# The inverse of a chunked scan gets a scheduling priority on VectorE, ScalarE and the queues, and the clock that merges its streams gets other pauses

## The chip, the cores and the metric

The kernel runs on one core of a Trainium2 chip. The metric is the device time of one execution in microseconds (us), from the first to the last instruction, with what lies around them. Times of a program are medians over several runs.

## What is computed

The reference is two layers of a block with 256 latent and 256 context tokens (512 columns here), width 1024. Each layer is a SwiGLU half step, a mixer of three branches (grouped attention, RWKV-7 in both directions, neighbourhood attention) and a second SwiGLU half step. The change touches the RWKV branch alone. Cut to what matters:

```python
def rwkv_scan(state0, xs, emit):
    def step(state, inp):
        r_t, w_t, k_t, v_t, a_t, b_t = inp
        sa = jnp.einsum('zbhvk,zbhk->zbhv', state, a_t)
        state = state * w_t[..., None, :] + sa[..., :, None] * b_t[..., None, :] + v_t[..., :, None] * k_t[..., None, :]
        out = jnp.einsum('zbhvk,zbhk->zbhv', state, r_t) if emit else None
        return state, out
    return lax.scan(step, state0, xs)
```

It runs for two directions z, 8 heads of 64. In layer 0 all 512 tokens give an output, in layer 1 the 256 latent tokens alone.

## The kernel before, in words

The scan is computed in chunks of 64 tokens (8 per direction), and the 8 heads as four pairs, ct = 0 to 3 (here "blocks"). For each block and direction the kernel makes scaled keys and rates (`rwkv_dir`, L1119 to L1177, mostly VectorE, DVE), Gram matrices of 64x64 (`gram`, L1205), the inverse of one minus a triangular matrix per chunk, and then the chain over the 8 chunks (`chain_steps`, L1365), which is the only part that runs chunk after chunk.

The inverse has two parts. `blocks16` (L1270) takes the 16x16 diagonal blocks through DRAM into another layout, solves them with 30 short instructions on DVE (L1284, L1286), and takes them back. `inverse` (L1293) then doubles the block size twice: for each direction z it builds T and W (L1310, two instructions), and runs a sequence that goes back and forth between TensorE (PE) and DVE: PE `ps_x` into X (DVE L1327), PE `ps_it` into T (L1331), PE `ps_iw` into W (L1334), then PE 32x32 groups `ps_x2` (L1345, in the rows `ps_x`) and `ps_w2` (L1354, in the rows `ps_w`), each copied by ScalarE (ACT, L1240) and DVE (L1242) halves. All PSUM results of one direction share one or two banks, so the next group also needs the one before to be read out.

Around it lie other works. `rwkv_proj` (L1045) projects keys k, values v and r of the next blocks: 24 matmuls `ps_p` each (L330 to L332), whose weights are split in two parts by ACT and DVE (`phi`, `plo`, L336 and L337), and whose result `shift` (L892 to L895) reads out. `rwkv_unit` (L1052) squares k on ACT (L1063), sums the squares on PE (`ps_ss`, L392) and normalises. `fill` pops a quantum of three matmuls `ps_gate` (L845 to L847) of a projection that is needed only after the scan; its weights come with `wload` (ACT L320, DVE L321).

The order on PE is written by hand. Each of these works is a Python generator that writes instructions and yields (cost, pause): the PE time of what it wrote and the time in which it expects its input not to be there. The class `Streams` keeps a clock, takes the first stream in the list whose pause is over, and otherwise one fill quantum, for which it adds 0.9 (layer 0) or 0.65 (layer 1) to the clock. PE executes in that order, and waits where an input is late. After the last chain the fill quanta that are left are written (all but 64 in layer 0 and 16 in layer 1), so the sum of PE work does not depend on the pauses. The quantum order is fixed, too.

```python
        streams = [chains(), inverses(), keys(), outs(), preps(), projections()]
        with self.tc.manual_schedule(engines={mybir.EngineType.PE}):
            while mix.step(streams):
                pass
        self.fill(len(self.fq) - left)
```

The other engines and the DMA queue have no order by hand: the scheduler of the framework orders them from the data dependencies, its own estimates and a priority, which is the place in the program. `self.prio(n)` (L339) gives what is written under it the priority of something written n instructions earlier. Before, of the scan only `chains()` writes under such a priority (200).

Of the kernel before, what the change touches and what calls it, by code (L numbers as in the profile page):

```python
# [7 lines left out]
F32 = mybir.dt.float32  # L8
F32R = mybir.dt.float32r
AF = mybir.ActivationFunctionType  # L10
# [4 lines left out]
P = 128  # L15
# [4 lines left out]
NT = SEQ + CTX  # L20
# [5 lines left out]
C = 64  # L26
# [86 lines left out]
class Program:  # L113
# [788 lines left out]
    def rwkv(self):  # L902
# [94 lines left out]
        def keys():  # L997
            for ct in range(4):
                yield from until("gram", ct)
                yield from until("chain", ct - 1)  # L1000
                yield from self.keys(sts[ct]["z"][1])
                done["keys"] = ct

        def inverses():
            for ct in range(4):
                yield from until("gram", ct)
                yield from blocks(ct)
                done["inverse"] = ct

        def chains():  # L1010
            for ct in range(4):
                yield from until("inverse", ct)
                yield from until("keys", ct)
                with self.prio(200):
                    po = self.bank("po", [P, NCH, C], "ps_oo")
                steps = self.chain_steps(sts[ct], po)
                while True:
                    with self.prio(200):
                        try:
                            s, *said = next(steps)  # L1020
                        except StopIteration:
                            break
                    if s == NCH // 2:
                        done["half"] = ct
                    yield said
                with self.prio(200):
                    sts[ct]["o"] = self.rp.tile([P, NT], F32, tag="yf", name="yf", bufs=1)
                    nc.scalar.activation(out=sts[ct]["o"][:, tok], in_=po.rearrange("p j t -> p (j t)")[:, tok],
                                         func=AF.Copy)
                done["chain"] = ct  # L1030

        def outs():
            yield from until("rates", 0)
            for ct in range(4):
                yield from until("chain", ct)
                yield from self.rwkv_out(ct, sts[ct])
                done["out"] = ct

        streams = [chains(), inverses(), keys(), outs(), preps(), projections()]
        with self.tc.manual_schedule(engines={mybir.EngineType.PE}):  # L1040
            while mix.step(streams):
                pass
# [2 lines left out]
    def rwkv_proj(self, ct, st, which):  # L1045

        i, full = dict(k=(T_RK, FULL), v=(T_RV, FULL), r=(T_R, self.tok))[which]
        pt = yield from self.proj(i + ct, full)
        st[which] = self.shift(i - T_R + ct, full, pt)
        yield 0.0, 2.5  # L1050

    def rwkv_unit(self, ct, st):  # L1052

        nc, l, tok, need = self.nc, self.l, self.tok, self.need
        pr = self.rwp[:, l]
        st["lora"] = self.rp.tile([P, 2, P], F32, tag="lora", name="lora", bufs=1)
        nc.sync.dma_start(out=st["lora"], in_=self.A["lora"][l, ct][:, 0:2, :])
        g2 = self.rp.tile([P, P], F32, tag="g2", name="g2")
        nc.sync.dma_start(out=g2, in_=self.A["lora"][l, ct][:, 2, :])
        yield lambda: "k" in st  # L1060
        k = st["k"]
        sq = self.t()
        nc.scalar.activation(out=sq, in_=k, func=AF.Square, scale=pr[:, 4, ct:ct + 1])  # L1063
        bc = yield from self.rstd_steps([sq], 4, self.hsel, 1.0, 1e-12)
        kk = self.rp.tile([P, NT], F32, tag="kk", name="kk", bufs=1)
        nc.vector.scalar_tensor_tensor(out=kk, in0=k, scalar=pr[:, 4, ct:ct + 1], in1=bc, op0=ALU.mult, op1=ALU.mult)
        st.update(g2=g2, kk=kk)
        yield 1.1, 0.2
# [31 lines left out]
    def rwkv_low(self, ct, st):  # L1100

        nc, l = self.nc, self.l
        lora = st["lora"]
        st["z"] = [None, None]
        st["pc"] = self.rp.tile([P, NCH, 2], F32, tag="pc", name="pc", bufs=2)
        st["low"] = [[], []]
        for i, (x, w) in enumerate(((self.wdt, 0), (self.adt, 2))):
            pts = [self.bank("aux", [P, NT], "ps_w") for _ in range(2)]
            for z in range(2):
                rows = slice(64 * z, 64 * z + 64)  # L1110
                nc.tensor.matmul(pts[z], lora[rows, i, :], x[rows, :], start=True, stop=True)
            for z in range(2):
                t = self.t()
                nc.scalar.activation(out=t, in_=pts[z], func=AF.Tanh, scale=0.5,
                                     bias=self.wah[:, l, w + z, ct:ct + 1])
                st["low"][z].append(t)
            yield 2.1, 0.0

    def rwkv_dir(self, ct, z, st):  # L1119

# [171 lines left out]
    def inverse(self, st, z, tag):  # L1292
# [4 lines left out]
        d, dr = st["z"][z], st["dr"]  # L1297
        G = d["G"]
        if z == 1:
            yield 0.0, 2.5  # L1300

        def ch(a):
            return a.rearrange("p (j t) -> p j t", t=C)
# [13 lines left out]
        def mm(name, a, b):  # L1317
            pt = self.bank(tag, [P, NCH, C], name)
            for j in range(NCH):
                for p, h in enumerate(halves):  # L1320
# [5 lines left out]
        X = ch(self.it())  # L1326
        nc.vector.tensor_tensor(out=X, in0=px, in1=self.mlev[:, z, :].unsqueeze(1).to_broadcast([P, NCH, C]),  # L1327
                                op=ALU.mult)
        yield 1.15, 1.6
        pt = mm("ps_it", lambda p, h, j: W[h, j, :], X)  # L1330
        nc.vector.tensor_tensor(out=T, in0=T, in1=pt, op=ALU.add)  # L1331
        yield 1.15, 0.0
# [318 lines left out]
```

## Time and profile before

| | |
|---|---|
| Median of 3 runs | 2953.67 us (2942.95 to 2959.11) |
| Profiled execution, its own time | 2946.8 us |
| Its span, first to last instruction | 2945.0 us |
| Mean granted TensorE clock | 0.953 |
| Busy PE, DVE, ACT, POOL | 93%, 58%, 36%, 11% |

A busy share of PE counts time in which a matmul was in flight. An idle stretch of PE ends when the last input of its next instruction arrives; the profile names the instruction that delivered it. The granted clock is 1.0 at 2.4 GHz and 0.5 at 1.2 GHz; TensorE has these two levels, and a mean between them tells the mix.

### The profile page before, as it was taken

How to read it: one execution, taken by the hardware profiler on the slowest of the kernel's cores; microseconds unless marked ns; L12 is line 12 of the kernel's file. 1: busy time of each engine (PE TensorE's matmuls, PEld its weight loads, DVE VectorE, ACT ScalarE, POOL GpSimd, SP SyncE). 2: the span in 40 equal slices, each digit the busy share in tenths (PEclk: the TensorE clock that was granted, in tenths of full speed). 3: DMA queues.
4: the chain of work that ended last, by engine and by line, in shares of the span. 5: the costliest groups of instructions: out<-in, count | busy, mean ns of one | idle time of the engine just before them, and what ended most of it. 6: DMA issues, size and time to landing. Idle time of an engine off the chain costs nothing. (4 is left out here: it accounts for less than half of the span.)

```text
span 2945.0 us, 48446 instructions
## 1 busy us (share of the span) xinstructions
PE 2733.0 (93%) x19654; PEld 2224.2 (76%) x19654; DVE 1716.8 (58%) x2855; ACT 1064.0 (36%) x1928; POOL 311.4 (11%) x306
## 2 busy tenths in 40 slices
PE   7999998898899899999999999999788899898998
PEld 5788886666667666697888878888666667877898
DVE  4667346666642357657762476533577774386664
ACT  3222234332322346442222332222543333464543
POOL 0000022111100101220000200001211110022000
PEclk9999998898899999999999999999888889999999
DMA  7655342221123533445553365433332113644654
GB/s 276 200 192 164 108 128 71 67 61 48 46 79 124 166 114 93 123 131 186 182 167 106 124 207 175 134 107 118 96 87 57 50 58 96 200 140 138 211 176 150
DMA packets 207616, 379.74 MB, mean 129 GB/s; under 512 B 80033, under 2 KB 110369, under 8 KB 207393
## 3 DMA queue, kind: packets, MB, share of 16 engines
q1 hardware_dynamic: 207392, 376.65, 41.1%
q8 instruction: 154, 2.52, 0.4%
q14 instruction: 70, 0.57, 0.1%
HBM read 342.50 MB, written 33.03 MB: 128 GB/s over the span
## 5 line engine op out<-in xcount | busy, mean ns | idle before, releaser
L320 ACT ACTIVATE whi<-raw 128x1024 fp32r<-128x1024 f32 (+1 forms) x399 | 415.2, 1041 | 1109.9 <-PE ps_o L331 297.3
L321 DVE TENSOR_TENSOR wlo<-raw,whi 128x1024 fp32r<-128x1024 f32 (+1 forms) x399 | 498.6, 1250 | 501.5 <-ACT whi L320 495.5
L330 PE MATMUL ps_o<-hh,whi 128*128 128x512 f32 (+1 forms) x770 | 268.8, 349 | 0.0
L253 DVE SCALAR_TENSOR_TENSOR acc<-araw,cs,acc 128x1024 f32<-128x1024 f32 x210 | 260.6, 1279 | 13.5 <-DMA araw<-in_w_ada 13.2
L845 PE MATMUL ps_gate<-uh,whi 128*128 128x512 f32 (+1 forms) x672 | 265.2, 395 | 3.2 <-ACT fg L851 2.7
L332 PE MATMUL ps_o<-hh,wlo 128*128 128x512 f32 (+1 forms) x770 | 267.9, 348 | 0.0
L331 PE MATMUL ps_o<-hl,whi 128*128 128x512 f32 (+1 forms) x770 | 266.6, 346 | 0.0
L330 PE MATMUL ps_fg<-uh,whi 128*128 128x512 f32 (+1 forms) x704 | 256.6, 364 | 7.6 <-ACT uh L336 3.8
L332 PE MATMUL ps_fg<-uh,wlo 128*128 128x512 f32 (+1 forms) x704 | 254.4, 361 | 6.2 <-DVE wlo L321 6.2
L332 PE MATMUL ps_fu<-uh,wlo 128*128 128x512 f32 (+1 forms) x704 | 251.9, 358 | 4.6 <-DVE wlo L321 4.6
L331 PE MATMUL ps_fg<-ul,whi 128*128 128x512 f32 (+1 forms) x704 | 253.6, 360 | 0.1
L330 PE MATMUL ps_fu<-uh,whi 128*128 128x512 f32 (+1 forms) x704 | 251.0, 356 | 0.9 <-ACT whi L320 0.9
L331 PE MATMUL ps_fu<-ul,whi 128*128 128x512 f32 (+1 forms) x704 | 250.9, 356 | 0.0
L846 PE MATMUL ps_gate<-ul,whi 128*128 128x512 f32 (+1 forms) x672 | 243.2, 362 | 0.0
L847 PE MATMUL ps_gate<-uh,wlo 128*128 128x512 f32 (+1 forms) x672 | 242.5, 361 | 0.0
L330 PEld LDWEIGHTS ps_fg<-uh,whi 128*128 128x128 f32 x704 | 135.2, 192 | 39.3 <-ACT whi L320 12.0
L330 PEld LDWEIGHTS ps_o<-hh,whi 128*128 128x128 f32 x770 | 144.7, 188 | 20.4 <-ACT whi L320 1.7
L331 PEld LDWEIGHTS ps_o<-hl,whi 128*128 128x128 f32 x770 | 144.5, 188 | 20.1
L332 PEld LDWEIGHTS ps_o<-hh,wlo 128*128 128x128 f32 x770 | 144.7, 188 | 18.2
L845 PEld LDWEIGHTS ps_gate<-uh,whi 128*128 128x128 f32 x672 | 132.0, 196 | 32.5 <-issue 5.7
L332 PEld LDWEIGHTS ps_fg<-uh,wlo 128*128 128x128 f32 x704 | 134.9, 192 | 27.1 <-DVE wlo L321 7.6
L332 PEld LDWEIGHTS ps_fu<-uh,wlo 128*128 128x128 f32 x704 | 133.7, 190 | 25.9 <-DVE wlo L321 7.2
(299 smaller groups left out, 5193.3 us busy)
## 6 DMA issues: line engine op xcount, KB each, us to landing
raw<-in_ffn_wi SPq DMA_DIRECT2D x176, 512.0 KB, 3.6
araw<-in_w_ada SPq DMA_DIRECT2D x144, 512.0 KB, 3.8
raw<-in_w_in SPq DMA_DIRECT2D x92, 512.0 KB, 3.7
raw<-in_ffn_wo SPq DMA_DIRECT2D x70, 448.0 KB, 3.3
raw<-in_ffn_wo SPq DMA_DIRECT2D x35, 512.0 KB, 3.5
pd<-fg SPq DMA_DIRECT2D x52, 256.0 KB, 2.0
raw<-in_w_branch SPq DMA_DIRECT2D x24, 512.0 KB, 3.7
raw<-in_w_in SPq DMA_DIRECT2D x44, 256.0 KB, 2.7
```

Of the source, the lines that this page charges most:

```text
L253: nc.vector.scalar_tensor_tensor(out=a, in0=raw, scalar=c, in1=a, op0=ALU.mult, op1=ALU.add)
L320: nc.scalar.activation(out=hi[:, :m], in_=r, func=AF.Copy)
L321: self.lo = nc.vector.tensor_tensor(out=lo[:, :m], in0=r, in1=hi[:, :m].bitcast(F32), op=ALU.subtract)
L330: nc.tensor.matmul(pt, wh, xh[k], start=first and k == 0, stop=False)
L331: nc.tensor.matmul(pt, wh, xl[k], start=False, stop=False)
L332: nc.tensor.matmul(pt, wl, xh[k], start=False, stop=last and k == n - 1)
L845: nc.tensor.matmul(pt, wh, xh, start=k == 0, stop=False)
L846: nc.tensor.matmul(pt, wh, xl, start=False, stop=False)
L847: nc.tensor.matmul(pt, wl, xh, start=False, stop=k == KD - 1)
```

## The change

It does three things. The streams `chains()` and `inverses()` are wrapped in `urgent`, so that all they write has a priority 600 and 400 instructions earlier (before: 200 for the chains, none for the inverse). Five pauses of the merging clock become longer, and one is added: after the square of k (`rwkv_unit`), 9.0 for the first block and 2.0 for others; `rwkv_proj` 5.0 for 2.5; the second group of `rwkv_low` 0.5 for 0.0; the start of the second direction's inverse 4.0 for 2.5; after X in the inverse 2.2 for 1.6. No arithmetic is added, removed or altered. Line numbers of the changed kernel are two or three higher in these functions.

```diff
--- before.py
+++ after.py
@@ -1007,26 +1007,28 @@
                 yield from blocks(ct)
                 done["inverse"] = ct
 
+        def urgent(n, stream):
+
+            while True:
+                with self.prio(n):
+                    try:
+                        said = next(stream)
+                    except StopIteration:
+                        return
+                yield said
+
         def chains():
             for ct in range(4):
                 yield from until("inverse", ct)
                 yield from until("keys", ct)
-                with self.prio(200):
-                    po = self.bank("po", [P, NCH, C], "ps_oo")
-                steps = self.chain_steps(sts[ct], po)
-                while True:
-                    with self.prio(200):
-                        try:
-                            s, *said = next(steps)
-                        except StopIteration:
-                            break
+                po = self.bank("po", [P, NCH, C], "ps_oo")
+                for s, *said in self.chain_steps(sts[ct], po):
                     if s == NCH // 2:
                         done["half"] = ct
                     yield said
-                with self.prio(200):
-                    sts[ct]["o"] = self.rp.tile([P, NT], F32, tag="yf", name="yf", bufs=1)
-                    nc.scalar.activation(out=sts[ct]["o"][:, tok], in_=po.rearrange("p j t -> p (j t)")[:, tok],
-                                         func=AF.Copy)
+                sts[ct]["o"] = self.rp.tile([P, NT], F32, tag="yf", name="yf", bufs=1)
+                nc.scalar.activation(out=sts[ct]["o"][:, tok], in_=po.rearrange("p j t -> p (j t)")[:, tok],
+                                     func=AF.Copy)
                 done["chain"] = ct
 
         def outs():
@@ -1036,7 +1038,7 @@
                 yield from self.rwkv_out(ct, sts[ct])
                 done["out"] = ct
 
-        streams = [chains(), inverses(), keys(), outs(), preps(), projections()]
+        streams = [urgent(600, chains()), urgent(400, inverses()), keys(), outs(), preps(), projections()]
         with self.tc.manual_schedule(engines={mybir.EngineType.PE}):
             while mix.step(streams):
                 pass
@@ -1047,7 +1049,7 @@
         i, full = dict(k=(T_RK, FULL), v=(T_RV, FULL), r=(T_R, self.tok))[which]
         pt = yield from self.proj(i + ct, full)
         st[which] = self.shift(i - T_R + ct, full, pt)
-        yield 0.0, 2.5
+        yield 0.0, 5.0
 
     def rwkv_unit(self, ct, st):
 
@@ -1061,6 +1063,7 @@
         k = st["k"]
         sq = self.t()
         nc.scalar.activation(out=sq, in_=k, func=AF.Square, scale=pr[:, 4, ct:ct + 1])
+        yield 0.0, 9.0 if ct == 0 else 2.0
         bc = yield from self.rstd_steps([sq], 4, self.hsel, 1.0, 1e-12)
         kk = self.rp.tile([P, NT], F32, tag="kk", name="kk", bufs=1)
         nc.vector.scalar_tensor_tensor(out=kk, in0=k, scalar=pr[:, 4, ct:ct + 1], in1=bc, op0=ALU.mult, op1=ALU.mult)
@@ -1114,7 +1117,7 @@
                 nc.scalar.activation(out=t, in_=pts[z], func=AF.Tanh, scale=0.5,
                                      bias=self.wah[:, l, w + z, ct:ct + 1])
                 st["low"][z].append(t)
-            yield 2.1, 0.0
+            yield 2.1, 0.5
 
     def rwkv_dir(self, ct, z, st):
 
@@ -1297,7 +1300,7 @@
         d, dr = st["z"][z], st["dr"]
         G = d["G"]
         if z == 1:
-            yield 0.0, 2.5
+            yield 0.0, 4.0
 
         def ch(a):
             return a.rearrange("p (j t) -> p j t", t=C)
@@ -1326,7 +1329,7 @@
         X = ch(self.it())
         nc.vector.tensor_tensor(out=X, in0=px, in1=self.mlev[:, z, :].unsqueeze(1).to_broadcast([P, NCH, C]),
                                 op=ALU.mult)
-        yield 1.15, 1.6
+        yield 1.15, 2.2
         pt = mm("ps_it", lambda p, h, j: W[h, j, :], X)
         nc.vector.tensor_tensor(out=T, in0=T, in1=pt, op=ALU.add)
         yield 1.15, 0.0
```

What it moves is seen in the order of the instructions on each engine. The first place is PE at the end of the first block's chain in layer 0, where the projection of k for the third block ends, too. `ps_u` is a step of the chain, `ps_ss` sums the squares of k, `ps_gate` is fill. Before:

```order
L330 MATMUL ps_p<-uh,phi 128x512
L331 MATMUL ps_p<-ul,phi 128x512
L332 MATMUL ps_p<-uh,plo 128x512
L1400 MATMUL ps_u<-zs,W 64x64 x4
L392 MATMUL ps_ss<-c_hsel,t 128x2 x4
L845 MATMUL ps_gate<-uh,whi 128x512
L846 MATMUL ps_gate<-ul,whi 128x512
L847 MATMUL ps_gate<-uh,wlo 128x512
L1420 MATMUL ps_oo<-G,X 64x64 x4
L330 MATMUL ps_p<-uh,phi 128x512
```

and now:

```order
L330 MATMUL ps_p<-uh,phi 128x512
L331 MATMUL ps_p<-ul,phi 128x512
L332 MATMUL ps_p<-uh,plo 128x512
L1403 MATMUL ps_u<-zs,W 64x64 x4
L845 MATMUL ps_gate<-uh,whi 128x512
L846 MATMUL ps_gate<-ul,whi 128x512
L847 MATMUL ps_gate<-uh,wlo 128x512
L845 MATMUL ps_gate<-uh,whi 128x512
L846 MATMUL ps_gate<-ul,whi 128x512
L847 MATMUL ps_gate<-uh,wlo 128x512
L1423 MATMUL ps_oo<-G,X 64x64 x4
L392 MATMUL ps_ss<-c_hsel,t 128x2 x4
L1193 MATMUL ps_kb<-c_ident,bk 128x64 x8
```

Six fill matmuls and four of the chain (`ps_oo`) now stand ahead of `ps_ss`; before it stood right behind `ps_u`.

The second place is PE in the inverse of the same layer's second block. `ps_v` and `ps_bo` belong to another stream, `ps_p` is a projection. Before:

```order
L1321 MATMUL ps_x<-it,G 64x64 x16
L1082 MATMUL ps_v<-c_center,sh 64x64 x16
L1095 MATMUL ps_bo<-bonus,c_hdiag 128x512
L1321 MATMUL ps_it<-it,W 64x64 x16
L1321 MATMUL ps_x<-it,G 64x64 x16
L1321 MATMUL ps_iw<-W,it 64x64 x16
L330 MATMUL ps_p<-uh,phi 128x512
L331 MATMUL ps_p<-ul,phi 128x512
L332 MATMUL ps_p<-uh,plo 128x512
L1321 MATMUL ps_it<-it,W 64x64 x16
L1345 MATMUL ps_x_5533<-it,G 32x32 x16
L1321 MATMUL ps_iw<-W,it 64x64 x16
L1354 MATMUL ps_w_5571<-W,it 32x32 x16
```

and now:

```order
L1324 MATMUL ps_x<-it,G 64x64 x16
L1085 MATMUL ps_v<-c_center,sh 64x64 x16
L1098 MATMUL ps_bo<-bonus,c_hdiag 128x512
L1324 MATMUL ps_it<-it,W 64x64 x16
L1324 MATMUL ps_iw<-W,it 64x64 x16
L1324 MATMUL ps_x<-it,G 64x64 x16
L330 MATMUL ps_p<-uh,phi 128x512
L331 MATMUL ps_p<-ul,phi 128x512
L332 MATMUL ps_p<-uh,plo 128x512
L1348 MATMUL ps_x_5562<-it,G 32x32 x16
L330 MATMUL ps_p<-uh,phi 128x512
L331 MATMUL ps_p<-ul,phi 128x512
L332 MATMUL ps_p<-uh,plo 128x512
L1324 MATMUL ps_it<-it,W 64x64 x16
L1357 MATMUL ps_w_5603<-W,it 32x32 x16
L1324 MATMUL ps_iw<-W,it 64x64 x16
```

The second `ps_x`, the start of the other direction, moved behind `ps_iw` of the first direction, and a second group of three `ps_p` stands between the groups of the inverse.

The third place is DVE during that inverse. `it` and `W` from `ps_x`, `ps_it` and `ps_iw` and the copies of 32 partitions belong to the inverse; `t`, `ar`, `bk`, `pj`, `pc` are `rwkv_dir` for the next block. Before:

```order
L1169 TENSOR_SCALAR t<-t,c_rwp,ka_3353 128x512
L1327 TENSOR_TENSOR it<-ps_x,c_mlev 128x512
L1173 TENSOR_TENSOR bk<-t 128x8x64
L1175 SCALAR_TENSOR_TENSOR t<-t,kk 128x512
L1131 SCALAR_TENSOR_TENSOR t<-scan_3375,t 128x512
L1176 TENSOR_TENSOR bk<-t 128x8x64
L1139 TENSOR_TENSOR t<-t 128x512
L1334 TENSOR_TENSOR W<-W,ps_iw 128x512
L1142 TENSOR_TENSOR t<-t 128x512
L1331 TENSOR_TENSOR it<-it,ps_it 128x512
L1242 COPY it<-ps_x_5533 32x256
L1334 TENSOR_TENSOR W<-W,ps_iw 128x512
```

and now:

```order
L1091 COPY X<-ps_v 64x8x64
L1337 TENSOR_TENSOR W<-W,ps_iw 128x512
L1172 TENSOR_SCALAR t<-t,c_rwp,ka_3353 128x512
L1330 TENSOR_TENSOR it<-ps_x,c_mlev 128x512
L1176 TENSOR_TENSOR bk<-t 128x8x64
L1178 SCALAR_TENSOR_TENSOR t<-t,kk 128x512
L1245 COPY it<-ps_x_5562 32x256
L1179 TENSOR_TENSOR bk<-t 128x8x64
L1334 TENSOR_TENSOR it<-it,ps_it 128x512
L1134 SCALAR_TENSOR_TENSOR t<-scan_3375,t 128x512
L1245 COPY W<-ps_w_5603 32x8x32
L1337 TENSOR_TENSOR W<-W,ps_iw 128x512
```

W of the first direction (L1334 before, L1337 now) stood behind X of the second direction (L1327) and five instructions of `rwkv_dir`; now it stands ahead of that X (L1330). In `blocks16` the 30 short instructions keep their neighbours.

## Rows read from the trace of the kernel before

**Rows 1.** The page, part 1: busy us, share of the span, instructions.

```profile
PE 2733.0 (93%) x19654; PEld 2224.2 (76%) x19654; DVE 1716.8 (58%) x2855; ACT 1064.0 (36%) x1928; POOL 311.4 (11%) x306
```

**Rows 2.** Both scans, windows: PE, PEld, DVE, ACT, POOL busy, PEclk, DMA, GB/s.

```profile
426.00:914.30 488.30, 428.68 (x4540) 319.76 (x4541) 300.45 (x656) 171.52 (x356) 68.73 (x64) 0.91 0.24 68
2065.70:2507.80 442.10, 380.62 (x4344) 304.85 (x4345) 286.33 (x650) 168.48 (x358) 66.41 (x63) 0.88 0.26 75
```

**Rows 3.** Waits of PE, whole run: waiter, releaser: us in total, times, longest.

```profile
PE ps_ss L392 <- ACT t L1063: 27.6, 8, 5.3
PE ps_it L1321 <- DVE it L1327: 11.4, 5, 4.6
...
PE ps_p L332 <- DVE plo L337: 6.7, 2, 4.5
PE ps_w L1354 <- ACT it L1240: 6.3, 7, 1.1
...
PE ps_x L1321 <- DVE it L1310: 5.3, 2, 4.1
PE ps_first L330 <- DMA raw<-in_w_in: 5.3, 1, 5.3
...
PE ps_x L1345 <- DVE W L1334: 4.7, 2, 3.8
...
PE ps_x L1321 <- ACT t L1144: 4.0, 1, 4.0
...
PE ps_p L330 <- ACT sh L893: 3.7, 2, 2.2
...
PE ps_w L1354 <- DVE it L1242: 3.5, 6, 1.5
PE ps_first L330 <- ACT wG L320: 3.3, 1, 3.3
...
PE ps_x L1321 <- DVE bonus L1096: 2.2, 2, 1.2
...
PE ps_x L1345 <- DVE G L1227: 1.4, 2, 0.8
PE ps_iw L1321 <- DVE it L1331: 1.4, 1, 1.4
```

**Rows 4.** Timeline of PE, layer 0: start, length, form, count [idle before].

```profile
637.75 1.11 PE L392 MATMUL ps_ss<-c_hsel,t 128*128 128x2 f32 x8 [3.91 <-ACT t L1063]
```

**Rows 5.** Timeline of PE, inverse of the second block, layer 0.

```profile
662.40 1.15 PE L1321 MATMUL ps_x<-it,G 64*64 64x64 f32 x32 [1.22 <-DVE bonus L1096]
...
670.59 1.07 PE L1345 MATMUL ps_x<-it,G 32*32 32x32 f32 x32 [3.83 <-DVE W L1334]
671.59 1.97 PE L1321 MATMUL ps_iw<-W,it 64*64 64x64 f32 x32
```

**Rows 6.** Timeline of DVE, same stretch.

```profile
664.79 0.68 DVE L1327 TENSOR_TENSOR it<-ps_x,c_mlev 128x512 f32<-128x512 f32 x1
666.32 0.69 DVE L1173 TENSOR_TENSOR bk<-t 128x512 f32<-128x512 f32 x1 [0.85 <-POOL t L1171]
...
669.85 0.68 DVE L1334 TENSOR_TENSOR W<-W,ps_iw 128x512 f32<-128x512 f32 x1
```

**Rows 7.** Timeline of PE, fill of 512 columns, layer 0.

```profile
687.88 0.39 PE L845 MATMUL ps_gate<-uh,whi 128*128 128x512 f32 x1
688.11 0.39 PE L846 MATMUL ps_gate<-ul,whi 128*128 128x512 f32 x1
```

**Rows 8.** Timeline of PE, fill of 256 columns, layer 1.

```profile
2201.47 0.28 PE L845 MATMUL ps_gate<-uh,whi 128*128 128x256 f32 x1
2201.59 0.28 PE L846 MATMUL ps_gate<-ul,whi 128*128 128x256 f32 x1
```

**Rows 9.** Windows: inverse and chain of the second block, layer 0.

```profile
651.50:681.50 30.00, 24.09 (x386) 16.82 (x380) 21.87 (x40) 13.12 (x28) 4.49 (x3) 0.80 0.12 30
682.00:731.00 49.00, 42.95 (x533) 31.36 (x533) 37.48 (x89) 13.26 (x33) 6.46 (x5) 0.99 0.23 66
```

## The prediction

> **What bounds the kernel now.** I read the page's busy shares first. TensorE (PE) is busy for 93% of the span and VectorE (DVE) for 58% [rows 1], so a change elsewhere pays only where PE stands still. The windows of the two scans come next [rows 2]. The reader should see two things there. PE is busy for 428.7 of 488.3 us and for 380.6 of 442.1 us, so it is idle for 59.6 and 61.5, together 121.1 us. And the granted clock is 0.91 and 0.88 in these windows, against 0.953 over the whole run. No engine is full there: DVE is busy for 300 of 488 us. What is short is neither work nor bandwidth but an input at the right moment. The waits of PE then say which inputs [rows 3].
>
> PE's order is fixed and the sum of its work does not depend on the pauses, because fill matmuls remain behind the last chain in both orders (345 and 390 of them before, 300 and 315 now). So a pause that is longer than needed costs next to nothing, and one that is too short costs the wait. The time falls by what PE idles less, and by what its clock gives back. It does not fall by a shorter scan as such.
>
> **The change, part by part.**
>
> *The pauses after the square of k and after a projection.* The wait for the square (L1063) is the longest in the list: 27.6 us in 8 times [rows 3]. One of them is 3.91 us [rows 4]; the others are of that kind, apart from one short one per layer, whose place also gets work put ahead. Now six fill matmuls stand ahead in the three later blocks of layer 0, six to nine in those of layer 1. A fill matmul of 512 columns starts 0.23 us after the one before [rows 7], one of 256 columns 0.12 us [rows 8]. That is 3 x 6 x 0.23 = 4.1 us and 3 x 7 x 0.12 = 2.5 us, together 7. Some chain groups move ahead as well, which I do not count. What remains is the same wait, about 2.5 us long where it was 3.9. Bounds: nothing, if the square comes later by as much; 27.6, if all is covered.
>
> *The inverse.* Nine rows of the waits belong to it (L1321, L1345, L1354): 11.4 + 6.3 + 5.3 + 4.7 + 4.0 + 3.5 + 2.2 + 1.4 + 1.4 = 40.2 us in eight inverses [rows 3], 5.0 each. The second block of layer 0 shows how they come about: 1.22 and 3.83 us [rows 5]. During the longer one DVE goes from X (L1327) at 664.79 through five instructions of rwkv_dir to W (L1334) at 669.85, 5.1 us later [rows 6]. W reads the bank that the 32x32 group on PE needs. In the new order W stands ahead of that X, and a group of three projection matmuls (0.7 us by [rows 7]) separates the steps on PE. Nothing is taken off DVE. W then waits for its own matmuls and for one or two instructions of 0.7 us [rows 6], so I leave 1 us of the 5 and gain 4 in this block. The second and third blocks of both layers have the same mixture on DVE: 4 x 4 = 16 us. In the first blocks the new order still has three to six instructions of rwkv_dir between steps of the inverse, so I take half of 5.0 for these two, 5 us. In the last blocks no rwkv_dir is left to overtake: 0. Sum 21, bounds 0 and 40. blocks16 itself gains nothing: its 30 instructions keep their neighbours.
>
> What is late next is rwkv_dir for the following block, by three or four instructions of 0.7 us. The Gram group of the first direction waits for it, and the chain is queued behind that group on PE. I cost this at nothing. Its cover: the `bk` which that group reads stands on DVE ahead of the inverse's last copies, and the chain cannot start without those. If the cover is gone, that is the slower rival below. The small loads and stores of the inverse also pass weight loads on the DMA queue, and its ACT copies of G pass splits of weights. Both I cost at nothing, too, because fill, whose weights come later, can wait in three raw buffers; without that cover the rows on `ps_gate` would grow waits.
>
> *The first stretch of each scan.* The added pause of 9.0 lets the 24 matmuls of r move in among the first projections. These waited 3.3 and 5.3 us for weights [rows 3]. 24 x 0.23 = 5.5 us covers the first wait, 24 x 0.12 = 2.9 us a part of the second: 6 us gained. Against it, the next projections arrive sooner at weights whose split (plo, L337) stands on DVE behind rwkv_dir, and at a bank that `shift` must read out (L893). These waits were 6.7 + 3.7 us, and 5.5 and 2.9 us of work no longer stand ahead of them. At worst they grow by 8.4. I take half, 4, since no row shows how much earlier DVE gets there. Net gain 2, between -2 and 8.
>
> *The clock.* In the window of the inverse the granted clock is 0.80 over 30.0 us, a loss of 6.0; in the chain behind it, with few waits, it is 0.99 [rows 9]. The price shows on one form: 32 matmuls of 64x64 take 1.15 us at the upper level (2.4 GHz) and 1.97 at the lower (1.2 GHz), right behind the wait of 3.83 us [rows 5]. PE was busy for 24.1 of the 30 us, so at most 0.2 x 24 = 4.8 us can come back. With short waits left I take half, 2.4, in the four inner blocks: 10 us. Bounds: 0, and 8 x 4.8 = 38.
>
> *Sum.* 7 + 21 + 2 + 10 = 40 us. The profiled execution took 2946.8 us, so 2906.8 by its own time. The median of the runs shown is 6.9 us above it, and 2953.7 - 40 = 2914 us is the forecast, 1.4% faster.
>
> **The rivals.**
>
> *The clock stays low.* The waits shrink, but the inverse is a series of short groups with pauses between them, and PE falls to 1.2 GHz just the same. For it: the group behind the wait ran at the lower level [rows 5], and short waits remain in the inverse. Against it: the chain is a series of short groups too, with fill between them, and has 0.99 [rows 9]. The time would be 2914 + 10 = 2924. The Trainium skill bears on this: "TensorE: Matmul & The Clock Gate", section "A second HAM failure mode: psum-queue depth-cycling", describes a PE that idles briefly but often between groups of matmuls and swings between its two rates for that alone. By that rule the term of 10 us is nothing; the chain's 0.99 speaks against it, the inverse's 0.80 for it.
>
> *The waits change their names.* DVE was the last to deliver in most of these rows, and it has the same instructions as before. X of the second direction still stands behind rwkv_dir in the new order. Then the inverse's wait goes from L1334 to L1327, the 40 us stay, and only 7 and some 3 of the first stretch are won: 2953.7 - 10 = 2944.
>
> *The priority moves nothing that matters.* If what PE waits for is latency between engines, not the queue on DVE, the pauses alone act: 7 + 2, 2945. Against it speaks the 5.1 us on DVE with five foreign instructions in it [rows 6].
>
> *Slower.* rwkv_dir, overtaken, comes too late for the Gram group of the next block, which sits at the head of the chain on PE. The inverse has some seven DVE instructions that can pass, 7 x 0.69 = 4.8 us. There are six inverses with an rwkv_dir beside them: 29 us. A wait at that place would also pull the clock down where it is 0.99 now, 4.8 us each by the inverse's loss: 29 more. Against it stand 7 + 21: 58 - 28 = 30, so 2984. It decides from a new wait of (7 + 21) / 6 = 4.7 us per block. What speaks against it is the DVE order, in which the first `bk` still precedes the inverse's end.
>
> **How the numbers follow.** The forecast has 0.50, the low clock 0.20, the renamed waits 0.17, the idle priority 0.05, slower 0.05, and 0.03 is left for a gain of over 66 us. The range reaches on the good side to 7 + 30 + 8 + 21 = 66 us (three quarters of the inverse's waits, the best first stretch, over half of the clock's bound): 2888. On the other side it takes in the renamed waits: 2944. A measurement of this kernel tells about 0.5%, 15 us, from no change. Under 2939 lie the forecast, the low clock, the large gain and a third of the renamed waits: 0.80. Within 0.5% lies the rest without the slower case: 0.15. Slower: 0.05.
>
> **What would show it.** In the changed profile the row for the square of k should fall from 27.6 to about 20 us, and the nine rows of the inverse from 40 to about 19. PE's idle time in the two scans should fall from 121 to about 91, and the granted clock in the inner inverses should rise from 0.80 towards 0.9. The row on plo may grow. The prediction is wrong if the inverse's rows keep their sum under other names, if `ps_g` or the chain's `ps_u` show new waits of over 4 us, or if the time falls without PE's idle time falling.

## The result, and the profile after

The changed kernel takes 2908.5 us (median of 4 runs, 2904.1 to 2911.4), the kernel before 2953.8 in the runs beside it. The ratio is 0.985, with a 95% interval of 0.982 to 0.988: 45 us less. The forecast was 2914, its range 2888 to 2944. The profiled execution took 2911.3 us with a span of 2909.5, against 2946.8 and 2945.0 before. Two of the six executions of the kernel called e6 below took 6465 and 13190 us and are left out as slow runs.

The page of the changed kernel, part 1, first engine (to compare with [rows 1]):

```profile
PE 2721.4 (94%) x19654; PEld 2214.0 (76%) x19654; DVE 1716.9 (59%) x2855; ACT 1063.5 (37%) x1928; POOL 310.2 (11%) x306
```

The same number of instructions stands on each engine, as it must. The windows of the two scans of the changed kernel answer to [rows 2], in the same columns:

```profile
425.30:905.20 479.90, 432.92 (x4585) 321.41 (x4586) 302.46 (x657) 175.11 (x360) 68.54 (x63) 0.93 0.25 72
2047.60:2478.70 431.10, 382.32 (x4419) 306.86 (x4420) 290.34 (x653) 172.23 (x364) 66.12 (x63) 0.90 0.28 81
```

PE is idle for 47.0 and 48.8 us, 95.8 where it was 121.1, and the granted clock went from 0.91 and 0.88 to 0.93 and 0.90. These windows do not hold the same work, since more fill runs inside the scan now. For equal work the reader takes another pair: from the first projection of a scan to the first matmul of the attention behind it, when all fill has run. First the kernel before:

```profile
426.10:1024.50 598.40, 529.65 (x5005) 401.97 (x5006) 331.17 (x691) 203.08 (x400) 75.85 (x68) 0.91 0.28 84
2065.70:2585.50 519.80, 449.36 (x4880) 370.95 (x4880) 320.62 (x692) 201.15 (x408) 74.16 (x69) 0.89 0.32 94
sum 1118.20, PE 979.01 PEld 772.92 DVE 651.79 ACT 404.23 POOL 150.01; mean PE 489.51 PEld 386.46 DVE 325.90 ACT 202.12 POOL 75.00
```

and the changed one:

```profile
425.30:1001.40 576.10, 520.63 (x5006) 392.80 (x5006) 330.72 (x691) 203.91 (x400) 75.76 (x68) 0.94 0.30 88
2047.60:2548.90 501.30, 442.48 (x4880) 364.32 (x4880) 320.86 (x692) 200.27 (x408) 73.86 (x69) 0.90 0.33 97
sum 1077.40, PE 963.11 PEld 757.12 DVE 651.58 ACT 404.18 POOL 149.62; mean PE 481.56 PEld 378.56 DVE 325.79 ACT 202.09 POOL 74.81
```

With one matmul more or less in 9885, the length falls by 40.8 us. PE's idle time (length less busy) falls from 139.2 to 114.3, by 24.9. The same matmuls take 15.9 us less, and that is the clock. These two numbers, idle and busy over equal work, carry the rest of the text. (Between the scans, where no code changed, this execution took 5 us more than the one before; so the two profiled executions lie 35.5 us apart.)

The waits of PE in the changed kernel, whole run (waiter, releaser: us in total, times, longest), answer to [rows 3]:

```profile
PE ps_ss L392 <- ACT t L1065: 15.8, 6, 3.4
PE ps_iw L1324 <- DVE it L1334: 9.7, 8, 2.3
...
PE ps_p L330 <- ACT sh L893: 4.8, 3, 3.2
...
PE ps_w L1357 <- DVE G L1230: 3.9, 2, 2.6
PE ps_p L332 <- DVE plo L337: 3.6, 1, 3.6
PE ps_x L1348 <- DVE W L1337: 3.0, 3, 1.9
PE ps_p L330 <- ACT phi L336: 2.8, 1, 2.8
PE ps_g L1226 <- DVE G L1230: 2.4, 2, 2.1
...
PE ps_x L1324 <- DVE it L1313: 2.1, 1, 2.1
PE ps_w L1357 <- DVE it L1245: 2.1, 5, 0.7
PE ps_g L1226 <- DVE X L1091: 2.1, 1, 2.1
...
PE ps_it L1324 <- DVE it L1330: 0.8, 1, 0.8
PE ps_first L330 <- ACT wG L320: 0.6, 1, 0.6
```

The square's row fell from 27.6 to 15.8. The inverse's rows (`ps_x`, `ps_it`, `ps_iw`, `ps_w`, with three of 0.5, 0.3 and 0.2 that are not shown) sum to 22.6 us, against 40.2. What is left there has another name: `ps_iw` stands directly behind `ps_it` now and waits for T (L1334). The wait of the first projections for a weight DMA (5.3) is gone, and plo fell from 6.7 to 3.6. Small waits of the Gram groups, `ps_g`, came up, the longest 2.1 us, and fill (`ps_gate`) now waits 2.8 us for its weights (L321).

The second block's inverse in layer 0, the place of [rows 5], in the timeline of PE (start, length, form, count, idle before):

```profile
656.49 1.15 PE L1324 MATMUL ps_it<-it,W 64*64 64x64 f32 x32
659.25 1.15 PE L1324 MATMUL ps_iw<-W,it 64*64 64x64 f32 x32 [1.62 <-DVE it L1334]
660.23 1.10 PE L1324 MATMUL ps_x<-it,G 64*64 64x64 f32 x32
662.15 0.69 PE L1348 MATMUL ps_x<-it,G 32*32 32x32 f32 x32
```

and in that of DVE, to be read against [rows 6]:

```profile
658.52 0.68 DVE L1334 TENSOR_TENSOR it<-it,ps_it 128x512 f32<-128x512 f32 x1
...
660.60 0.67 DVE L1337 TENSOR_TENSOR W<-W,ps_iw 128x512 f32<-128x512 f32 x1
661.20 0.53 DVE L1172 TENSOR_SCALAR t<-t,c_rwp,ka 128x512 f32<-128x512 f32 x1
661.65 0.68 DVE L1330 TENSOR_TENSOR it<-ps_x,c_mlev 128x512 f32<-128x512 f32 x1
```

W (L1337) stands ahead of X (L1330) now, and the 32x32 group that reads that bank starts without a wait, where it waited 3.83 us. All groups of this inverse run at the upper level: 64x64 in 1.15 us, where [rows 5] has 1.97 behind the wait.

### The profile page after: what moved, and what is told of

It reads as the page before. It is cut to its first block, busy times and chain, and to the rows that moved or that the text cites. A ratio compares the mean times of both kernels' runs of the same rounds, so it can differ in the third digit from the quotient of the medians.

```text
span 2909.5 us, 48424 instructions
## 1 busy us (share of the span) xinstructions
PE 2721.4 (94%) x19654; PEld 2214.0 (76%) x19654; DVE 1716.9 (59%) x2855; ACT 1063.5 (37%) x1928; POOL 310.2 (11%) x306
## 4 chain that ended last, share of the span: by engine, by line
PE 43%; DVE 5%; DMA 3%; ACT 2%; issue 2%; POOL 1%; SPq 0%; POOLq 0%; ACTq 0%; DVEq 0%
PE ps_o L330 3%; PE ps_o L332 3%; PE ps_o L331 3%; PE ps_fu L332 3%; PE ps_fg L330 3%; PE ps_fu L331 3%; PE ps_fu L330 3%; PE ps_fg L332 3%; PE ps_fg L331 3%; PE ps_gate L845 2%; PE ps_gate L846 1%; PE ps_gate L847 1%; DMA araw<-in_w_ada 1%; PE ps_ss L424 1%; DVE wlo L321 1%
## 5 line engine op out<-in xcount | busy, mean ns | idle before, releaser
L321 DVE TENSOR_TENSOR wlo<-raw,whi 128x1024 fp32r<-128x1024 f32 (+1 forms) x399 | 498.7, 1250 | 496.5 <-ACT whi L320 490.5
```

The source lines that it names most:

```text
L321: self.lo = nc.vector.tensor_tensor(out=lo[:, :m], in0=r, in1=hi[:, :m].bitcast(F32), op=ALU.subtract)
```

## The experiments

Twelve kernels were run, each timed beside the kernel before. In the table, "idle" and "busy" are PE's over the two windows of equal work; "first" is the idle part of the two stretches from a scan's first projection to its first `ps_x` of the inverse; "inverse" is the idle part of the eight inverses, each from its first `ps_x` to its last `ps_w`. All four come from one profiled execution each, in us, and such an execution can lie up to 12 us from its kernel's median (e3); that of the kernel before lies 7 us below its own. Between the scans, where all kernels have the same code, PE's busy time differs by up to 6 us from one execution to another (1017.4 before, 1023.7 in e1). So these columns tell where time went, and the ratio how much; a few us in one of them show nothing. The sums behind the last two columns are, for the kernel before, first stretches and then inverses,

```profile
sum 272.00, PE 226.74 PEld 183.48 DVE 175.21 ACT 125.26 POOL 59.22; mean PE 113.37 PEld 91.74 DVE 87.60 ACT 62.63 POOL 29.61
...
sum 162.80, PE 123.14 PEld 104.97 DVE 117.92 ACT 63.25 POOL 13.36; mean PE 15.39 PEld 13.12 DVE 14.74 ACT 7.91 POOL 1.67
```

and for the changed one

```profile
sum 256.60, PE 227.20 PEld 184.11 DVE 168.93 ACT 124.00 POOL 57.41; mean PE 113.60 PEld 92.06 DVE 84.46 ACT 62.00 POOL 28.70
...
sum 147.80, PE 121.69 PEld 101.09 DVE 119.65 ACT 63.91 POOL 14.45; mean PE 15.21 PEld 12.64 DVE 14.96 ACT 7.99 POOL 1.81
```

| kernel | ratio to before (95%) | idle | busy | first | inverse |
|---|---|---|---|---|---|
| before | 1 | 139.2 | 979.0 | 45.3 | 39.7 |
| the change | 0.985 (0.982 to 0.988) | 114.3 | 963.1 | 29.4 | 26.1 |
| e1 priority alone | 0.9955 (0.9938 to 0.9972) | 134.7 | 968.6 | 47.6 | 29.4 |
| e2 pauses alone | 0.9904 (0.9887 to 0.9921) | 126.8 | 968.9 | 29.2 | 41.8 |
| e3 pauses outside the inverse | 0.9925 (0.9904 to 0.9946) | 121.7 | 971.7 | 28.0 | 46.2 |
| e4 longer pauses | 0.9790 (0.9773 to 0.9808) | 95.6 | 964.0 | 24.7 | 27.1 |
| e5 inverse 400, chains 200 | 0.9837 (0.9813 to 0.9860) | 113.2 | 970.4 | 31.2 | 25.6 |
| e5b chains 600, inverse none | 0.9919 (0.9899 to 0.9938) | 124.6 | 978.4 | 33.0 | 38.7 |
| e6 longer pauses, old priorities | 0.9884 (0.9859 to 0.9910) | 114.5 | 975.7 | 24.9 | 43.8 |
| e8 two more pauses longer | 0.9776 (0.9751 to 0.9802) | 95.1 | 958.6 | 25.2 | 24.4 |
| e9 square 2.0 alone | 0.9980 (0.9965 to 0.9994) | 139.4 | 980.8 | 45.1 | 47.1 |
| e10 first block 9.0, projections 5.0 | 0.9965 (0.9951 to 0.9978) | 138.6 | 976.1 | 32.0 | 48.5 |
| e11 square 9.0 / 2.0 alone | 0.9927 (0.9905 to 0.9949) | 129.3 | 975.2 | 35.9 | 46.1 |
| e12 square 2.0, projections 5.0 | 1.0004 (0.9989 to 1.0018) | 142.1 | 985.9 | 46.9 | 45.7 |

**The two halves of the change.** e1 is the kernel before with the new priorities, e2 the kernel before with the new pauses, of which four are longer and one is added.

```diff
# e1, on the kernel before (with urgent() as in the change)
-        streams = [chains(), inverses(), keys(), outs(), preps(), projections()]
+        streams = [urgent(600, chains()), urgent(400, inverses()), keys(), outs(), preps(), projections()]
# e2: the five hunks of the change with a yield, and nothing else
```

> The kernel before with the new priorities (600 for the chains, 400 for the inverse) and all pauses as before. PE's order is then that of the kernel before, instruction for instruction; only VectorE, ScalarE, GpSimd and the queues are reordered. Theory 1 (the inverse waited in VectorE's queue): the nine wait rows of the inverse fall from 40 to about 20 us, the square's wait stays at 27 us, PE's idle time in the scans falls from 121 to about 100 us, time about 2928 us. Rival (the pauses did it all): the inverse's rows stay over 35 us, time within 8 us of the kernel before.

> The kernel before with the five new pauses and the old priorities. PE's order is then that of the changed kernel, instruction for instruction. Theory 1: the square's wait falls to about 16 us as in the changed kernel, the inverse's rows stay at 32 us or more because VectorE's queue still holds it up, time about 2933 us. Rival (the pauses did it all): the inverse's rows fall to about 22 us as in the changed kernel, time about 2910 us.

The windows of equal work, first e1:

```profile
sum 1103.30, PE 968.63 PEld 761.69 DVE 654.29 ACT 404.74 POOL 150.22; mean PE 484.31 PEld 380.84 DVE 327.15 ACT 202.37 POOL 75.11
```

then e2:

```profile
sum 1095.70, PE 968.90 PEld 763.20 DVE 649.49 ACT 405.23 POOL 148.10; mean PE 484.45 PEld 381.60 DVE 324.75 ACT 202.62 POOL 74.05
```

The priority gives 0.45% and the pauses 0.96%; the product of the ratios is 0.986, so the halves add up to the whole. They act in different places. The priority takes 10 us of idle time out of the inverses and none out of the first stretches; the pauses take 16 us out of the first stretches and none out of the inverses. Not all of that stays: PE's idle time as a whole falls by 4.5 us in e1 and by 12.4 in e2, since other waits grew. Each half has matmuls that are 10 us shorter in its profile, both together 15.9. In e1 the inverse's rows of the waits fell from 40 to 28.4 us, where the first theory gave 20; in e2 they are 36.2 us and the square's row is 16.1, as it said. e1 took 2939.2 us and e2 2925.9; so the first theory had the order of the two halves the wrong way round: the priority is worth less than it said, the pauses more.

**Which priority.** e5 sets the chains back to 200, e5b takes the inverse's away.

```diff
-        streams = [urgent(600, chains()), urgent(400, inverses()), ...
# e5
+        streams = [urgent(200, chains()), urgent(400, inverses()), ...
# e5b
+        streams = [urgent(600, chains()), inverses(), ...
```

> The changed kernel with the chains' priority back at 200; the inverse keeps 400, the pauses are the new ones. The first theory says that it is the inverse's instructions on DVE that had to overtake rwkv_dir, so the chains' 600 is worth nothing: 2909, within 4 us of the changed kernel. The rival says that the chains' copies (X of the chain, out of ps_u and ps_h) needed the higher place, too: near the pauses alone, 2920 to 2926.

> The changed kernel without a priority for the inverse; the chains keep 600, the pauses are the new ones. The first theory: as the pauses alone, 2926, with the waits of ps_iw and ps_it for DVE at 19 us as there. The rival (it is the chains' priority that works): 2909 to 2913.

e5 has 2908.3 us, the changed kernel's time; e5b has 2931.8, no better than the pauses alone, and its waits of `ps_iw` and `ps_it` for `it` on DVE sum to 18.1 us, close to the 19 expected. So, beside the new pauses, the inverse's 400 does all that the priorities do. That it works through DVE's order, and not through ACT or the queue, which are reordered as well, is read from these rows; no run separates the three. Nor were higher priorities run.

**Which pause.** e3 has the pauses outside the inverse; e9 to e12 take it apart.

```diff
# e3: the hunks of rwkv_proj, rwkv_unit and rwkv_low, on the kernel before
# e9, on the kernel before
+        if ct:
+            yield 0.0, 2.0
# e10: 5.0 in rwkv_proj, 0.5 in rwkv_low, and
+        if ct == 0:
+            yield 0.0, 9.0
# e11, on the kernel before
+        yield 0.0, 9.0 if ct == 0 else 2.0
# e12: e9 and
-        yield 0.0, 2.5
+        yield 0.0, 5.0
```

> The kernel before with only the three pauses outside the inverse (after the square of k, after a projection, in the second group of rwkv_low), no priority, the inverse's pauses as before. Theory 1: only the square's wait falls (27.6 to about 16 us) and the waits at the first projections shift; with some clock given back, time about 2940 us. Rival (the first stretch and the square carry most of the gain): time under 2930 us.

e3 took 2931.1 us, 9 less than the first theory gave it and 1 more than the rival's bound, so its pauses were taken one by one.

> The kernel before with one edit: a pause of 2.0 after the square of k in the blocks after the first. The first theory says that this pause is most of what e3 gained, because the square's waits are seven long ones: the row of L1063 falls from 27.6 to 16, and with the clock it gives 14 of e3's 23 us: 2940. The rival says that the sum of e3 comes from the first stretch (the 9.0 and the 5.0): then here the row falls as well, but the waits go to the inverse, and the time is 2950 or above.

> The kernel before with the other pauses of e3: 9.0 after the square in the first block, 5.0 for 2.5 after a projection, 0.5 in rwkv_low. The first theory: first stretch and projections are 9 of e3's 23 us, 2945, with the row of the square at about 25 and no waits left for the first projections' weights (8.6 us of ps_first in the kernel before). The rival: 18 us or more, 2937 or below; the prediction's 2 us: 2952.

e9 brought the row of the square down as expected, and 6 us of time, not 14. Its waits of PE show where the rest went:

```profile
PE ps_ss L392 <- ACT t L1063: 16.6, 8, 4.0
PE ps_iw L1323 <- DVE it L1333: 11.6, 5, 3.6
```

The square's row is 11 us shorter, but PE's idle time is what it was, 139.4 us, and that of the inverses rose from 39.7 to 47.1. (The 6 us by which the medians differ are no more than the 7 us by which the profiled execution of the kernel before was short.) This was neither theory's number: the rival had the place right (the waits go to the inverse), and its time of 2950 lies 2 us above the 2948.3 that were measured. e10 gave 10 us, as the first theory had it, with the square's row at 24.7 us, but e9 and e10 together did not make e3's 23. So two pairs were run.

> The kernel before with the added pause alone (9.0 in the first block, 2.0 in the others), no longer pause after a projection. Together e9 and e10 gained 16 us of e3's 23. One reading: the parts simply add, the rest is noise; then this is 2943 (6 for the square, 5 or so for the first stretch). The other: each wait removed shifts everything behind it, and only a pause after both the projection and the square keeps the waits from going to the inverse; then this is 2947 or above, with the inverse's rows at 45 us or more.

> The kernel before with 2.0 after the square in the later blocks and 5.0 after a projection. If the parts simply add, 2943 to 2946. If the pair is what makes e3, 2933 to 2936, with the inverse's rows no higher than the 40 us of the kernel before.

Neither reading held. e11, the added pause alone, is worth as much as e3. e12 is worth nothing. So the longer pause after a projection gains nothing on top of the square's 2.0, and the 9.0 in the first block gains much: e11 less e9 is 0.5%, some 15 us. It does not do so alone, for e10 has it without the 2.0 and gives 10 us, while e3, which is e10 with the 2.0, gives 23. The table suggests why the parts are worth more together. In e9, in e10 and in e3 alike the inverses idle for 46 to 48.5 us, 7 to 9 more than before: each part alone loses that much there, and both together lose it once. The first stretches of e9, both layers,

```profile
sum 267.20, PE 222.06 PEld 180.31 DVE 169.78 ACT 122.82 POOL 58.04; mean PE 111.03 PEld 90.16 DVE 84.89 ACT 61.41 POOL 29.02
```

and of e11

```profile
sum 272.60, PE 236.68 PEld 192.39 DVE 175.64 ACT 127.94 POOL 56.97; mean PE 118.34 PEld 96.19 DVE 87.82 ACT 63.97 POOL 28.48
```

show it: in e11 PE does 14.6 us more work there and is idle for 35.9 us, not 45.1. In the table every kernel with the 9.0 has at most 35.9 in that column, every kernel without it at least 45.1.

**Longer pauses.** After the change, 15.8 us were left at the square and 9.7 at `ps_iw`. e4 lengthens these two pauses; e6 is e4 with the old priorities; e8 is e4 with two more.

```diff
# e4, on the changed kernel
-        yield 0.0, 9.0 if ct == 0 else 2.0
+        yield 0.0, 9.0 if ct == 0 else 4.5
...
         nc.vector.tensor_tensor(out=T, in0=T, in1=pt, op=ALU.add)
-        yield 1.15, 0.0
+        yield 1.15, 1.0
# e8: e4, 2.6 for 1.4 behind ps_x2, 4.0 for 2.5 behind the output's square
```

> The changed kernel with two pauses longer still: 4.5 for 2.0 after the square of k in the later blocks, and 1.0 for 0.0 after ps_it in the inverse, where the changed kernel shows a new wait of ps_iw for T (9.7 us in 8 times). Theory 1: a wait that a pause covers with fill is won, so the square's wait falls from 15.8 to about 5 us and the wait of ps_iw to about 2, time about 2895 us. Rival (the scan is bound by its latencies, the same time is waited for elsewhere): PE's idle time in the scans stays at 96 us, time about 2908 us.

> The longer pauses of e4 (4.5 after the square, 1.0 after the T step) with the old priorities. The first theory says that priority and pauses remove different waits, since a fixed pause cannot know how many foreign instructions stand ahead of W on DVE: e4's 2891 + 16 = 2907, with 8 us or more of waits of the inverse for DVE that e4 does not have. The rival says that the priority was worth something only where a pause was too short, so that with long pauses it is worth little: 2891 to 2896.

> e4 with two more pauses lengthened: 2.6 for 1.4 after ps_x2 (the rows of ps_w in e4 are 16.8 us in 17 waits) and 4.0 for 2.5 before the sum of squares of the output (5.5 us in 4 waits). The first theory (a pause longer than needed costs next to nothing): the 22 us of these rows fall to 8, and the clock gives some back: 2891 - 14 - 3 = 2874. The rival: the waits go to other names, or the later chain delays what follows: 2888 to 2894.

e4 took 2890.8 us (2887.9 to 2896.7). Its waits of PE:

```profile
PE ps_w L1357 <- DVE it L1245: 9.8, 10, 2.2
PE ps_w L1357 <- ACT it L1243: 7.0, 7, 1.1
...
PE ps_ss L392 <- ACT osq L1433: 5.5, 4, 1.7
...
PE ps_ss L392 <- ACT t L1065: 2.2, 3, 1.1
```

The square's wait is all but gone, and here the time followed: idle 95.6 us. The busy time did not fall any further (964.0 against 963.1), so e4's gain shows as idle time. Inside the inverses, though, nothing was gained: waits of the 32x32 groups came up in place of those of `ps_iw`, and the inverses idle for 27.1 us, not 26.1. Outside them PE idles 19.7 us less, which is where the longer pause after the square acts; the two pauses were not run apart.

With the old priorities the same pauses give 2916.0 to 2928.7 us, e2's time: e6 is 0.94% behind e4. So the priority is worth about twice as much under long pauses as under the old ones, against both theories' numbers. The waits of e6 show why:

```profile
PE ps_x L1322 <- DVE it L1311: 12.5, 3, 5.6
PE ps_it L1322 <- DVE it L1328: 8.1, 5, 3.6
```

These are the inverse's first and second group, waiting for T and X on DVE. The square's wait is 2.2 us there as in e4, but the inverses idle for 43.8 us and not 27.1, which is most of the 18.9 us of idle time between the two. Against e2, which has the same priorities, e6 idles 12.3 us less, and its time is not clearly better (0.9884 and 0.9904, with intervals that overlap).

e8's lengthened pauses did what they were meant to, in its waits of PE:

```profile
PE ps_w L1357 <- DVE it L1245: 2.5, 5, 0.8
...
PE ps_ss L392 <- ACT osq L1433: 1.7, 2, 1.4
```

The 22.3 us of these places in e4 (9.8 + 7.0 + 5.5) are 4.7 (with 0.5 of `ps_w` for the ACT copies, not shown), yet its 2889.7 us are e4's time: PE idles 95.1 us, not 95.6. Other waits grew, as the rival said; the longest is a new one of 5.0 us of `ps_it` for the output stream on DVE (`yf`, L1443). e4 is the version to keep, 0.6% ahead of the changed kernel.

## Why the prediction was right, point by point

*The sum.* It said 40 us and the windows of equal work show 40.8. Its forecast case is the one that came: PE idles less in the inverses, at the square and in the first stretch, and its clock rises. It said 121 to 91 us of idle time in the scans; it was 95.8. But all four terms have the wrong size, and the errors cancel, so that the total was met so closely is luck in part. The 24.9 us of idle time are 15.9 in the first stretches and 13.6 in the inverses, less 4.6 that came up elsewhere.

*The pauses after the square: 7 us.* The row fell by 11.8, by more than was taken; 5.2 of that lie in the first stretches, where it fell from 11.6 to 6.4. Outside the first stretches and the inverses the row fell by 6.6, yet PE's idle time rose there by 4.6 (54.2 to 58.8). That the row's microseconds are time was never shown, and e9 speaks against it: alone, the pause takes 11 us off the row, nothing off PE's idle time in its profile, and 6 us off the median. The prediction's premise that a wait covered by fill is time won holds only if what comes next is not late, too. At the square it held in e4; in e9 and e8 most of the wait came back at other inputs, and e11's inverses idle nearly as long as e9's (46.1 and 47.1).

*The inverse: 21 us.* The rows fell by 17.6, the idle time inside the inverses by 13.6, and e1, e5 and e5b show that it was the inverse's priority that did it; that it acted on DVE, as argued from W behind X and rwkv_dir [rows 6], fits the rows. The four inner blocks were not alike, though. Their windows before, second and third block of layer 0, then of layer 1:

```profile
656.80:679.10 22.30, 16.39 (x362) 13.37 (x361) 16.14 (x32) 8.93 (x21) 1.51 (x2) 0.78 0.07 22
752.10:776.00 23.90, 17.36 (x362) 14.21 (x361) 17.09 (x33) 10.80 (x23) 1.64 (x2) 0.77 0.11 31
...
2277.70:2298.70 21.00, 15.71 (x349) 14.11 (x347) 16.22 (x32) 8.23 (x19) 4.02 (x3) 0.76 0.05 14
2362.90:2384.30 21.40, 15.58 (x363) 13.68 (x361) 19.07 (x39) 8.74 (x20) 2.54 (x2) 0.81 0.13 41
```

and in the changed kernel:

```profile
653.30:670.50 17.20, 14.77 (x368) 11.84 (x367) 16.04 (x31) 8.82 (x20) 1.26 (x1) 1.00 0.06 20
745.50:762.10 16.60, 14.76 (x368) 11.83 (x367) 15.43 (x29) 8.19 (x19) 1.27 (x1) 1.00 0.04 13
...
2249.90:2269.30 19.40, 15.88 (x355) 13.86 (x355) 15.38 (x32) 7.60 (x18) 2.40 (x3) 0.79 0.08 8
2337.30:2359.50 22.20, 15.94 (x372) 13.56 (x371) 18.75 (x34) 9.62 (x22) 3.54 (x3) 0.79 0.07 14
```

In layer 0 the idle time of the two falls from 12.5 to 4.3 us, 4 each as forecast, and the clock rises to 1.00. In layer 1 it goes from 11.1 to 9.8, and the clock stays at 0.79. The step that failed is "4 x 4": it gave 9.5 us and not 16, 8.2 of them in layer 0. The place that was read closely was one block of layer 0, and the same gain was assumed for layer 1.

*The first stretch: 2 us, between -2 and 8.* This is the mis-sized step. The idle time there fell from 45.3 to 29.4 us, and e9 and e11 tie 9 us of it to the 9.0. Of these 15.9 us, 5.2 are the square's and were priced there. The working counted two waits for weights, 6 us of them; they fell by 8.0 (5.3 to nothing, 3.3 to 0.6). It charged 4 us for plo and shift. Most of that charge was not needed: plo fell from 6.7 to 3.6, L893 rose by 1.1, and 2.8 on phi came up, 1 us more in all. Left out were the other, smaller waits of a stretch in which PE was idle for 22.8 and 22.5 us, which fell by some 7 together. And fill, whose weights were put at nothing, waits 3.2 us for them there (`ps_gate`, 2.8 of it for L321, in e2 as well, so that comes with the pauses and not with the priority). The views that were read [rows 2, 3] show the scans as a whole. A window over the stretch alone would have shown more than a third of the scans' idle time in it.

*The clock: 10 us, bounds 0 and 38.* 15.9 us came back in the windows of equal work, a figure that one execution tells to some 6 us. In the inner inverses of layer 0 all of it came back, where half was taken; in those of layer 1 nothing. That is not a matter of their waits alone, for in e5, which has the changed kernel's pauses and time, these two idle for 3.9 and 6.0 us, too, and have 0.87 and 0.91:

```profile
2251.20:2269.40 18.20, 14.32 (x355) 12.27 (x355) 15.39 (x32) 7.75 (x19) 2.42 (x3) 0.87 0.08 9
2336.90:2356.90 20.00, 14.01 (x372) 11.70 (x371) 18.49 (x34) 9.66 (x22) 3.07 (x2) 0.91 0.04 12
```

Outside, the front pauses may bring some: e3, which changes nothing in the inverse, is busy for 7.3 us less, little more than the spread between executions. The rival "the clock stays low" fell for layer 0 and is open for layer 1. The rule of the Trainium skill that stood beside it ("TensorE: Matmul & The Clock Gate", section "A second HAM failure mode: psum-queue depth-cycling") describes a kernel whose PE idles briefly between groups often enough that it swings between its rates. The trace does not show that for layer 0, where an inverse with a wait of 1.62 us and some shorter ones has a mean of 1.00, and does not exclude it for layer 1, where idle times of 3.5 and 6.3 us go with 0.79.

*The waits that would change names, and the slower case.* As a whole they did not come: no wait at `ps_g` is above 2.1 us, and none at `ps_u` showed. In parts they did. `ps_g` rose from 1.3 to 8.3 us in all its rows. Of these, 1.7 wait for `bk` of rwkv_dir and 2.1 for the tokens' X (L1091, 0.4 before): the mechanism of the slower rival, at about an eighth of the 29 us that it gave to these waits. The rest waits for copies of the Gram groups themselves (2.4), for the inverse's last copies and for ACT. And e9 and e8 are the renamed waits in pure form.

What stays open: why layer 1's inner inverses keep their waits. In the third block there, the 32x32 copy of the second direction stands behind a scan, a copy of tokens and a product of rwkv_dir on DVE even with the priority; whether its input came too late to overtake was not tried. Nor is it settled why a pause at the square sends its wait on to the inverse; e11 does that as e9 does, and what it gains beyond e9 (idle 129.3 for 139.4 us) is won in the first stretches (35.9 for 45.1). Nor is it known what sets the clock in layer 1's inner inverses, or was a kernel tried that gives the clock back without removing the waits.

## What to carry to other kernels

A wait that is covered by other work is time won only if the next input of the same chain is not late as well; compare PE's idle time over equal work, not the row of the wait. Where an engine's order is written by hand and its feeder's is not, the two must be set together: here the pauses cleared the entry of the scan, the priority cleared the queue on DVE, and longer pauses gained clearly (0.985 to 0.9790) only with the priority (0.9904 to 0.9884 without). Divide a scan's idle time by stretch before pricing an edit: the stretch at its start, some 30% of its length, held 37% of the idle time and gave 15.9 us of it, the inverses 13.6.

## What the runs showed of the hardware

The granted clock rose where waits went, but the idle time of a stretch alone does not set it. The inverse of the second block of layer 0, with nearly as many matmuls, runs at 0.78 with 5.9 us of idle time in 22.3 and at 1.00 with 2.4 in 17.2. With the priority alone (e1) it idles for 5.1 us and runs at 0.98:

```profile
656.60:675.30 18.70, 13.61 (x362) 11.08 (x361) 16.51 (x31) 8.74 (x20) 1.76 (x2) 0.98 0.08 26
```

Less idle time does not bring shorter matmuls everywhere, either: e4 has 19 us less of it than the changed kernel, and its matmuls take as long (964.0 and 963.1 us), as far as one execution of each can tell. In the two profiles of the change, about 40% of what it gained in the scans (15.9 of 40.8 us) came as shorter matmuls, not as shorter waits, so a sum over waits alone would have been a good third too small.
